# Up-projections of a hybrid attention trunk: split products for fp32, and a plan made from other durations

## The chip, the cores and the metric

The kernel runs on one core of one Trainium2 chip. The metric is the device time of one execution in microseconds (us), as the median of several runs.

## The reference

Two decoder layers work on 256 tokens of width 1024, all in fp32. In each layer the normed input goes through one wide projection (`w_in`), whose parts feed two attentions, NSA (compressed, selected and windowed keys) and MoBA, and two gates. The two attention outputs go through an up-projection each, are gated and summed, and go through `w_out`; a SwiGLU network follows.

```
for l in range(2):
    sh_m, sc_m, g_m, sh_f, sc_f, g_f = split(silu(c) @ w_ada[l] + b_ada[l], 6)
    h = rms_norm(x, norm_mix[l]) * (1.0 + sc_m) + sh_m
    (q_a, ..., q_b, k_b, v_b, g_br) = split(h @ w_in[l], ...)
    y_a = nsa_mixer(...)                       # 256 x 512
    y_b = moba_mixer(q_b, k_b, v_b, ...)       # 256 x 512
    gate_a, gate_b = split(sigmoid(g_br), 2)
    merged = gate_a * (y_a @ w_up_nsa[l]) + gate_b * (y_b @ w_up_moba[l])
    x = x + g_m * (merged @ w_out[l])
    h = rms_norm(x, norm_ffn[l]) * (1.0 + sc_f) + sh_f
    gt, up = split(h @ w_ffn_in[l], 2)
    x = x + g_f * ((silu(gt) * up) @ w_ffn_out[l])
```

## The kernel before, in words

Tokens are handled as two tiles of 128 (`t` = 0, 1), and nearly all time goes into products of a 128x128 piece of activations with a weight tile of 512 columns. Nearly all weights come in units of 128x2048 fp32 values (1 MB) into a tile `raw`. Most products are **split products**: ScalarE makes `hi`, the weights rounded to fp32r, VectorE makes `lo` = `raw` - `hi`, the activations are split alike, and `mm3` issues three fp32r matmuls in place of one fp32 matmul: high by high, high by low, low by high. A unit marked *whole* skips this: `part` multiplies `raw` itself in fp32. Whole are every second block of the lead-in, three units of layer 0, and all up-projections of both layers (`u = load_unit(A[w][l][:, cs_], 4, 512, True)`). The attention output of a token tile, in PSUM tile `y`, is copied to a quarter of the tile `yy` by one `evac` (`whole_piece`), on ScalarE or VectorE.

SBUF holds an arena of 17 tiles of 8 KB per partition. `raw` has the slots 0, 1, 2 (and 11 for some units); `hi` and `lo` have three slots each (and two more for units with `spare`), used by all split weights; `yy` has 11, 12, 13 or 14.

The program first records every operation (`Op`) with a cost in us. `order` then places them on the engines, always the one that can start first, ties by rank. `rounds` repeats this 60 times: each plan is replayed 8 times with random delays of transfers, operations ahead of a wait of TensorE are raised in rank, and the plan with the shortest replay is kept. So the costs written in `_vec`, `act`, `softmax_T` and so on decide the order on each engine, and which of two or three engines takes an operation. Loads go through SyncE's queue in that order; the dot products that make the modulation rows (`aw`, `ada_dot` on VectorE, 80 of them) are loaded and computed far ahead of their use, wherever the plan finds room.

In the last product of the last layer the last output block (token tile 1, columns 512 to 1023) is computed as two halves of 256 columns, so that the first half's residual can be finished while the second half's matmuls run.

Lines of the profile: L662 is a matmul of `term` (all weight products), L648 one of `mm` (attention), L669 a transpose, L583 and L589 VectorE with two tensors (L589 with a scalar too), L601 VectorE with one tensor, L631 ScalarE's `act`, L640 and L641 the two sides of `evac`, L678 a DMA.

Of the kernel before, what the change touches and what calls it, by code (L numbers as in the profile page):

```python
# [17 lines left out]
P = 128  # L18
# [100 lines left out]
class Op:  # L119
    def __init__(self, no, alts, key):  # L120
        self.no, self.alts, self.key = no, alts, key
        self.preds, self.succs, self.acc, self.new = {}, [], [], []
        self.bytes = 0
        self.level = 0.0
        self.stage, self.first, self.boost = None, False, 0.0
        self.func, self.loads, self.parts, self.paced, self.then = None, None, False, False, None
# [5 lines left out]
FIRST = 1000.0  # L132
LAT = {"PE": 0.24, "DVE": 0.09, "ACT": 0.09, "POOL": 0.2, "SP": 0.0, "Q": 0.0}
# [5 lines left out]
class Program:  # L139
# [9 lines left out]
    SWITCH = (0.0, 0.0, 0.1)  # L149
# [116 lines left out]
    def order(self):  # L266
# [24 lines left out]
        parts = False  # L291
# [43 lines left out]
        while left:  # L335
# [6 lines left out]
            for op in ready:  # L342
                if "SP" in op.alts and op.no != loads[0] and (op.paced or self.ops[loads[0]].stage == "lead"):
                    continue
                pl = place(op)
                if pl is None:
                    continue
                for e, (c, _) in op.alts.items():
                    est = max(free[e], pl[0],
                              max((f if q == e else f + LAT[q] for f, q in rt[op.no].values()), default=0.0))  # L350
                    if e == "PE" and op.parts != parts:
                        est = max(est, free[e] + self.SWITCH[0])
                    per.setdefault(e, []).append((est, op, pl[1], c))
# [4 lines left out]
            for e, cs in per.items():  # L358
# [3 lines left out]
                else:  # L362
                    w = eps[e] + (self.SWITCH[1] if e == "PE" else 0.0)
                    pick = max((c for c in cs if c[0] <= t0 + w), key=lambda c: (c[1].rank(e), -c[1].no))
# [38 lines left out]
            if e == "PE":  # L403
                parts = op.parts
# [14 lines left out]
            else:  # L419
                free[e] = t + c  # L420
# [21 lines left out]

    def fill(self, t0, t1):
# [15 lines left out]
        op.stage = "fill"  # L459
# [20 lines left out]
    def replay(self, steps, seed):  # L480
# [4 lines left out]
        dma, table, parts, gaps = 0.0, (), False, []  # L485
        for i, (e, op, c, deps) in enumerate(steps):
# [5 lines left out]
            if e == "PE":  # L492
                if op.stage != "fill" and op.parts != parts:
                    parts = op.parts
                    idle += self.SWITCH[2]
# [13 lines left out]
            free[e] = t + c  # L509
# [49 lines left out]
class Engines:  # L559
# [25 lines left out]
    def stt(self, out, a, s, b, op0, op1, accum=None):  # L585
# [5 lines left out]
                  [a, s, b], [out] + list(kw.values()), extra=0.08 if kw else 0.0)  # L591

    def ttr(self, out, a, b, op0, op1, init, accum):
        self._vec(("DVE",), cols(out), True,
                  lambda v: v.tensor_tensor_reduce(AP(out), AP(a), AP(b), 1.0, init, op0, op1, AP(accum)),  # L595
                  [a, b], [out, accum], extra=0.08)

    def ts(self, out, a, s1, s2, op0, op1=None, engs=("DVE",)):
# [3 lines left out]
                  [a, s1, s2], [out], psum=self._psum(a))  # L602
# [12 lines left out]
    def act(self, out, a, func, scale=None, bias=None, accum=None, late=()):  # L615
# [11 lines left out]
        if accum is not None:  # L627
            kw["accum_out"] = accum
            writes.append(accum)
            c += 0.2  # L630
# [12 lines left out]
    def mm(self, out, lhsT, rhs, start, stop, cost=None):  # L643
# [6 lines left out]
        op.parts = AP(lhsT).shape[0] < P or AP(out).shape[0] < P  # L650

    def term(self, out, lhsT, rhs, first):
# [13 lines left out]
        self.p.op({"PE": (cost, [go])}, [lhsT, rhs], [out], term=s)  # L666

    def tr(self, out, a, ident):
        self.p.op({"PE": (0.109, [lambda: self.nc.tensor.transpose(AP(out), AP(a), AP(ident))])}, [a, ident], [out])  # L669

    def dma(self, out, src, q="SP", least=60000):
# [5 lines left out]
        eng = {"SP": self.nc.sync, "POOL": self.nc.gpsimd}[q]  # L677
        return self.p.op({q: (0.43 if q == "SP" else 0.6, [lambda: eng.dma_start(AP(out), AP(src))])},  # L678
# [7 lines left out]

HALVED = 1
# [15 lines left out]
def trunk_kernel(tc, pools, A):  # L703
# [33 lines left out]
    NB = 17  # L737
# [16 lines left out]
    arena("yy", (11, 12, 13, 14), inturn=True)  # L754
# [373 lines left out]
    def lead_in(bs, h, W):  # L1128
# [16 lines left out]
        dma(vecs, A["vecs"], q="POOL")  # L1145
# [68 lines left out]
    def sublayer_mix(l, h):  # L1214
# [4 lines left out]
        ev, kv_, qv, vv, yv = (R.val(x_) for x_ in ("e", "kk", "qq", "ve", "yy"))  # L1219
# [185 lines left out]
        def softmax_T(s, t, nh, rq_small, cols_, gate):  # L1405
# [21 lines left out]
            alts["ACT"] = (nh * (0.295 + nk / 1200),  # L1427
# [47 lines left out]
        def nsa(t):  # L1475
# [43 lines left out]
            yaT[t] = whole_piece(quarter(yv, t, t), y)  # L1519

        def moba(t):
# [31 lines left out]
            ybT[t] = whole_piece(quarter(yv, 2 + t, 2 + t), y)  # L1553
# [72 lines left out]
        log_soon([yv, *tgv.values()])  # L1626
# [8 lines left out]
    def resid(l, t, c, b, g, e0=0, e1=512):  # L1635
# [3 lines left out]
        with R.ahead():  # L1639
            tt(r, b.of(e0)[:, e0:e1] if e1 - e0 < 512 else b, g[:, cs_], ALU.mult)  # L1640
# [6 lines left out]
    def sublayer_ffn(l, h):  # L1647
# [61 lines left out]
        full = (0, 512)  # L1709
        keys = [(*key, full) for key in keys]  # L1710

        parts = {(t, c): [full] for t in range(NT) for c in range(2)}
        if l == L - 1:
            parts[(NT - 1, 1)] = [(0, 256), (256, 512)]
            keys += [(i, t, k, c, e) for t in range(NT) for c in range(2) for e in parts[(t, c)]
                     for i in range(nu - nl, nu) for k in range(2)]
        else:
            keys += [(i, t, k, c, full) for t in range(NT) for i in range(nu - nl, nu) for k in range(2) for c in range(2)]
        for i, t, k, c, (e0, e1) in keys:
            kk = 2 * i + k  # L1720
            cs_ = slice(c * 512 + e0, c * 512 + e1)
            b = bs[(t, c)]
            if (e0, e1) != full:
                b = b.of(e0)[:, e0:e1]

            R.boost = 20.0 * (4 - 2 * t - c) - e0 / 50 if l == L - 1 and i >= nu - nl else 0.0
            mm3(b, aT[t][kk], us[i].hi[:, k, cs_], us[i].lo[:, k, cs_], kk == 0)
# [73 lines left out]
```

## Time and profile before

| | us |
|---|---|
| runs | 816.85, 816.95, 820.06 |
| median | 816.95 |
| span of the profiled execution | 815.4 |
| around the span (median - span) | 1.55 |
| TensorE busy | 803.8 (99%) |
| VectorE busy | 580.2 (71%) |
| ScalarE busy | 410.3 (50%) |
| DMA moved | 183.82 MB, 225 GB/s |

The span runs from the first to the last event of the program in the profiled execution; the page gives no other time of that execution, so the 1.55 us around it are the difference to the runs. A matmul's duration in a row is longer than its turn on the array, since matmuls overlap; what a kind of matmul costs is read from the distance between starts.

### The profile page before, as it was taken

To read this page: it belongs to the slowest core of one execution; us is meant where nothing else is said; L and a number is where in the kernel's file an instruction comes from. 1 tells how busy PE (TensorE), PEld (TensorE's weight loads), DVE (VectorE), ACT (ScalarE), POOL (GpSimd) and SP (SyncE) were. 2 spreads that over 40 slices of the span, in tenths; PEclk is the share of its full clock that TensorE was granted. 3 is DMA by queue.
4 is the path that set the end of the run, shared out by engine and by line. 5 is a ranking of instruction groups with operands and counts; after the bars stand their busy time and mean duration, and the time that the engine had idled before them with its cause. 6 is when DMAs were issued, how large, how long until landed. Compare 5 with 4: busy or idle time off the path is not lost.

```text
span 815.4 us, 10543 instructions
## 1 busy us (share of the span) xinstructions
PE 803.8 (99%) x3997; PEld 610.0 (75%) x3997; DVE 580.2 (71%) x1025; ACT 410.3 (50%) x654; POOL 79.5 (10%) x75
## 2 busy tenths in 40 slices
PE   8999999999999999999999999999999999999997
PEld 4567656764878888888878887676477888889886
DVE  6889977677986877777788898776377526545454
ACT  5445366662673534433585566587347524433441
POOL 4702620000100000000000442000000000000000
PEclk9999999999999999999999999999999999999999
DMA  9967585538949887977855785540391645555441
GB/s 357 416 230 290 161 295 182 175 130 310 372 152 338 311 305 288 327 293 259 311 174 214 278 289 180 188 151 25 104 344 69 210 153 174 202 192 207 151 158 52
DMA packets 74018, 183.82 MB, mean 225 GB/s; under 512 B 4304, under 2 KB 9696, under 8 KB 73456
## 3 DMA queue, kind: packets, MB, share of 16 engines
q1 hardware_dynamic: 73920, 183.08, 63.0%
q8 instruction: 31, 0.51, 0.2%
q14 instruction: 19, 0.16, 0.1%
q0 software_dynamic: 48, 0.08, 0.0%
HBM read 182.10 MB, written 1.05 MB: 225 GB/s over the span
## 4 chain that ended last, share of the span: by engine, by line
PE 88%; DVE 4%; DMA 2%; ACT 2%; POOL 2%; issue 1%; SPq 0%; DVEq 0%; POOLq 0%
PE bank L662 77%; PE bank L648 6%; PE bank L669 5%; DMA rows<-in_rows 1%; DVE tmp L583 1%; DMA raw<-in_w_out 1%; DVE lo L583 1%; POOL tmp L601 1%; DVE tmp L601 1%; ACT hp L631 1%; ACT hi L631 1%; SPq L678 0%; POOL tmp L583 0%; POOL at L1431 0%; DVE e L583 0%
## 5 line engine op out<-in xcount | busy, mean ns | idle before, releaser
L662 PE MATMUL bank<-hi,hp 128*128 128x512 f32 (+2 forms) x1296 | 359.2, 384 | 2.2 <-DVE hp L583 1.5
L583 DVE TENSOR_TENSOR lo<-raw,hi 128x2048 fp32r<-128x2048 f32 (+2 forms) x107 | 240.4, 2261 | 104.7 <-ACT hi L631 103.8
L631 ACT ACTIVATE hi<-raw 128x2048 fp32r<-128x2048 f32 (+2 forms) x107 | 200.6, 1891 | 223.1 <-PE bank L662 181.9
L662 PEld LDWEIGHTS bank<-hi,hp 128*128 128x128 f32 x1296 | 234.1, 188 | 59.1 <-issue 7.0
L662 PE MATMUL bank<-lo,hp 128*128 128x512 f32 (+2 forms) x648 | 208.2, 383 | 0.3 <-DVE lo L583 0.2
L662 PEld LDWEIGHTS bank<-lo,hp 128*128 128x128 f32 x648 | 119.3, 188 | 24.1 <-issue 2.6
L589 DVE SCALAR_TENSOR_TENSOR aw<-aw,crow 128x1024 f32<-128x1024 f32 x80 | 96.2, 1220 | 7.5 <-DMA aw<-in_w_ada 7.3
L662 PE MATMUL bank<-hi,aT 128*128 128x512 f32 (+1 forms) x364 | 100.7, 387 | 0.0
L662 PEld LDWEIGHTS bank<-hi,aT 128*128 128x128 f32 x364 | 66.6, 188 | 13.5 <-ACT hi L631 1.0
L662 PE MATMUL bank<-raw,yy 128*128 128x512 f32 x128 | 58.7, 596 | 0.7 <-ACT yy L640 0.7
L662 PE MATMUL bank<-lo,aT 128*128 128x512 f32 (+1 forms) x182 | 58.0, 385 | 0.0
L662 PE MATMUL bank<-raw,hd 128*128 128x512 f32 (+1 forms) x112 | 49.6, 568 | 0.9 <-ACT hd L631 0.9
L662 PEld LDWEIGHTS bank<-raw,yy 128*128 128x128 f32 x128 | 23.0, 190 | 23.7 <-issue 21.8
L662 PE MATMUL bank<-hi,mT 128*128 128x512 f32 x128 | 39.9, 403 | 0.1
L662 PEld LDWEIGHTS bank<-lo,aT 128*128 128x128 f32 x182 | 34.1, 188 | 6.1
L669 PE MATMUL bank<-ident,tmp 128*128 128x128 f32 x256 | 37.5, 274 | 1.2 <-DVE tmp L985 0.7
L631 ACT ACTIVATE at<-at,nb,rqa 128x128 f32<-128x128 f32 (+1 forms) x64 | 34.2, 536 | 7.5 <-DVE nb L589 7.5
L669 PEld LDWEIGHTS bank<-ident,tmp 128*128 128x128 f32 x256 | 30.4, 140 | 9.8 <-issue 1.8
L595 DVE CUSTOM_DVE_ANT_0 at<-bank,maskf 128x128 f32<-128x128 f32 (+1 forms) x96 | 29.5, 352 | 11.3 <-PE bank L669 8.9
L662 PEld LDWEIGHTS bank<-raw,hd 128*128 128x128 f32 x112 | 20.6, 189 | 17.2 <-issue 13.4
L583 DVE TENSOR_TENSOR tmp<-tmp,bank 128x512 f32<-128x512 f32 (+1 forms) x24 | 15.1, 639 | 22.0 <-PE bank L662 21.5
L631 ACT ACTIVATE tmp<-bank 128x512 f32<-128x512 f32 (+2 forms) x43 | 20.7, 509 | 16.3 <-PE bank L662 7.0
(185 smaller groups left out, 731.3 us busy)
## 6 DMA issues: line engine op xcount, KB each, us to landing
raw<-in_w_ffn_in SPq DMA_DIRECT2D x44, 1024.0 KB, 6.3
aw<-in_w_ada SPq DMA_DIRECT2D x80, 512.0 KB, 5.7
raw<-in_w_in SPq DMA_DIRECT2D x30, 1024.0 KB, 5.2
raw<-in_w_ffn_out SPq DMA_DIRECT2D x22, 1024.0 KB, 4.9
raw<-in_w_out SPq DMA_DIRECT2D x8, 1024.0 KB, 6.2
raw<-in_w_in SPq DMA_DIRECT2D x8, 908.0 KB, 9.1
sa<-in_w_ada SPq DMA_DIRECT2D x7, 1024.0 KB, 11.9
raw<-in_w_up_nsa SPq DMA_DIRECT2D x4, 1024.0 KB, 6.2
```

Of the source, the lines that this page charges most:

```text
L583: self._vec(engs, cols(out), True, lambda v: v.tensor_tensor(AP(out), AP(a), AP(b), op=op), [a, b], [out])
L589: lambda v: v.scalar_tensor_tensor(AP(out), AP(a), AP(s), AP(b), op0=op0, op1=op1, **{k: AP(x) for k, x in kw.items()}),
L595: lambda v: v.tensor_tensor_reduce(AP(out), AP(a), AP(b), 1.0, init, op0, op1, AP(accum)),
L601: lambda v: v.tensor_scalar(AP(out), AP(a), AP(s1), AP(s2), op0=op0, **kw),
L631: op = self.p.op({"ACT": (c, [lambda: self.nc.scalar.activation(AP(out), AP(a), func, **{k: AP(x) for k, x in kw.items()})])}, reads + lis ...
L648: op = self.p.op({"PE": (cost, [lambda: self.nc.tensor.matmul(AP(out), AP(lhsT), AP(rhs), start=start, stop=stop)])}, [lhsT, rhs], [out])
L662: self.nc.tensor.matmul(AP(out), AP(lhsT), AP(rhs), start=first, stop=v.gone == v.terms)
L669: self.p.op({"PE": (0.109, [lambda: self.nc.tensor.transpose(AP(out), AP(a), AP(ident))])}, [a, ident], [out])
```

## The change

It has five parts. (1) `UPS_WHOLE` is false for both layers, so the eight units of the up-projections are split like the others, and the attention output is split on the way out of PSUM (`y_pieces`): ScalarE writes the high part into `yy`, VectorE the low part into a second `yy` tile (`yl`). (2) The arena gets an 18th tile, first choice for `yy`; the scratch of software DMA is set to 2048 to make room. (3) The matmuls of the last output block run over 512 columns again; only its residual and its store stay in halves. (4) `vecs`, a table of constants of 81.5 KB, is loaded by ScalarE's queue and no longer by GpSimd's. (5) The planner gets other durations: VectorE and ScalarE instructions overlap by `OVER`, an accumulating one costs less, normalising the softmax on ScalarE costs less, VectorE scaling from PSUM by a column costs more, and a change of matmul shape on TensorE costs `TURN`, by row and column class (`forms`).

```diff
+OVER = {"PE": 0.0, "DVE": 0.08, "ACT": 0.1, "POOL": 0.0, "SP": 0.0, "Q": 0.0}
...
-    SWITCH = (0.0, 0.0, 0.1)
+    TURN, SLACK, TALL = 0.15, 0.0, 0.05
+    FLAT, STICK = (P, P), 0.0
...
-            if e == "PE":
-                parts = op.parts
+            if e == "PE" and op.forms:
+                if op.forms[0] != form:
+                    t = max(t, free[e] + self.turn(form, op.forms[0]))
+                form = op.forms[1]
...
-                free[e] = t + c
+                free[e] = t + c - OVER[e]
                 end = t + c
...
-        eng = {"SP": self.nc.sync, "POOL": self.nc.gpsimd}[q]
-        return self.p.op({q: (0.43 if q == "SP" else 0.6, [lambda: eng.dma_start(AP(out), AP(src))])},
+        eng = {"SP": self.nc.sync, "ACT": self.nc.scalar}[q]
+        return self.p.op({q: (0.43 if q == "SP" else 0.15, [lambda: eng.dma_start(AP(out), AP(src))])},
...
+UPS_WHOLE = (False, False)
...
-    NB = 17
+    NB = 18
...
-    arena("yy", (11, 12, 13, 14), inturn=True)
+    arena("yy", (17, 11, 12, 13, 14), inturn=True)
...
-        dma(vecs, A["vecs"], q="POOL")
+        dma(vecs, A["vecs"], q="ACT")
...
-        def whole_piece(d, src):
-            evac(d, src)
-            return [(None, None, d[:, j * P:(j + 1) * P]) for j in range(4)]
+        yl = None if UPS_WHOLE[l] else R.val("yy", dt=F32R)
+
+        def y_pieces(i, src):
+            d = quarter(yv, i, i)
+            if yl is None:
+                evac(d, src)
+                return [(None, None, d[:, j * P:(j + 1) * P]) for j in range(4)]
+            return split_into(d, quarter(yl, i, i), src)
...
-            alts["ACT"] = (nh * (0.295 + nk / 1200),
+            alts["ACT"] = (nh * (0.19 + nk / 1200) + 0.1,
...
-                u = load_unit(A[w][l][:, cs_], 4, 512, True)
+                u = load_unit(A[w][l][:, cs_], 4, 512, UPS_WHOLE[l])
...
-            keys += [(i, t, k, c, e) for t in range(NT) for c in range(2) for e in parts[(t, c)]
-                     for i in range(nu - nl, nu) for k in range(2)]
+            keys += [(i, t, k, c) for t in range(NT) for c in range(2) for i in range(nu - nl, nu) for k in range(2)]
...
-    nc = bacc.Bacc("TRN2", target_bir_lowering=False, num_devices=1)
+    nc = bacc.Bacc("TRN2", target_bir_lowering=False, num_devices=1, dynamic_dma_scratch_size=2048)
```

The order of instructions before and after differs nearly everywhere in its details. Three places matter here. In the names, `hp` is the split normed input, `kk`,`qq` are keys and queries, `pt` softmax weights, `ve` values, `at` softmax rows, `tg` gates, `mT` the gated sum; numbers tell buffers apart. The first place is TensorE in layer 0 at the first up-projections. Before:

```order
L662 MATMUL bank_64<-hi_1047,hp_322 128x512
L662 MATMUL bank_65<-raw_1155,yy_1177 128x512
L662 MATMUL bank_63<-raw_1155,yy_1177 128x512
L669 MATMUL bank_69<-ident_95,at_82 128x128 x4
L648 MATMUL bank_66<-kk_614,qq_682 128x256
...
L648 MATMUL bank_68<-pt_84,ve_772 64x128
L669 MATMUL bank_70<-ident_95,at_81 128x128 x4
L662 MATMUL bank_63<-raw_1155,yy_1177 128x512 x2
L662 MATMUL bank_64<-raw_1211,yy_1177 128x512 x2
L669 MATMUL bank_69<-ident_95,at_83 128x128 x4
```

And after:

```order
L659 MATMUL bank_68<-pt_85,ve_767 64x128
L659 MATMUL bank_68<-pt_84,ve_767 64x128
L678 MATMUL bank_63<-hi_1431,hp_318 128x512
L678 MATMUL bank_64<-hi_1431,hp_321 128x512
...
L678 MATMUL bank_63<-hi_1431,hp_321 128x512
L678 MATMUL bank_65<-hi_1492,yy_1117 128x512
L678 MATMUL bank_65<-lo_1508,yy_1117 128x512
L678 MATMUL bank_64<-hi_1492,yy_1117 128x512
L678 MATMUL bank_64<-lo_1508,yy_1117 128x512
L678 MATMUL bank_64<-hi_1492,yy_1258 128x512
```

Before, fp32 up-projections stand between the attention products of MoBA; after, gate products (`hi_1431`) fill that place, ten of them follow the last attention product, and the split up-projections come behind those, in one block. The second place is VectorE around the same point. Before, from the end of the last softmax:

```order
L613 RECIPROCAL ri_196<-rs_191 128x2
L589 SCALAR_TENSOR_TENSOR aw_74,mod_f_138<-aw_74,crow_101 128x1024
L589 SCALAR_TENSOR_TENSOR aw_72,mod_f_138<-aw_72,crow_101 128x1024
L583 TENSOR_TENSOR gcol_164<-gcol_164,vecs_104 128x8
L589 SCALAR_TENSOR_TENSOR aw_73,mod_f_138<-aw_73,crow_101 128x1024
L589 SCALAR_TENSOR_TENSOR tmp_78<-tg_978,bank_65 128x512
```

And after:

```order
L624 RECIPROCAL ri_196<-rs_191 128x2
L1450 TENSOR_TENSOR at_81<-at_81,ri_196 128x512
L593 TENSOR_TENSOR lo_1508<-raw_1217,hi_1492 128x2048
L652 COPY pt_85<-bank_69 128x512
L652 COPY pt_84<-bank_70 128x512
L593 TENSOR_TENSOR lo_1536<-raw_1260,hi_1516 128x2048
L599 SCALAR_TENSOR_TENSOR aw_72,mod_f_138<-aw_72,crow_101 128x1024
L593 TENSOR_TENSOR yy_1258<-bank_68,yy_1117 128x512
L599 SCALAR_TENSOR_TENSOR aw_73,mod_f_138<-aw_73,crow_101 128x1024
L593 TENSOR_TENSOR lo_1583<-raw_1470,hi_1570 128x2048
```

The low parts of the up-projection weights and of the attention output now stand where modulation dots (`aw`) stood, and fewer dots stand between them. The third place is the end of TensorE's program. Before, after the last transposes of activations:

```order
L669 MATMUL bank_69<-ident_95,tmp_75 128x128 x2
L662 MATMUL bank_66<-lo_5682,aT_5507 128x512
L662 MATMUL bank_66<-hi_5664,aT_5507 128x512 x2
...
L669 MATMUL bank_69<-ident_95,gcol_165 128x128 x4
L662 MATMUL bank_66<-hi_5679,aT_5629 128x256
...
L662 MATMUL bank_68<-hi_5765,aT_5751 128x512 x4
```

And after:

```order
L678 MATMUL bank_65<-lo_5499,hp_4811 128x256
L678 MATMUL bank_64<-lo_5805,aT_5747 128x512
L678 MATMUL bank_64<-hi_5795,aT_5747 128x512 x2
L685 MATMUL bank_69<-ident_95,tmp_76 128x128 x2
L678 MATMUL bank_64<-hi_5795,aT_5747 128x512
L685 MATMUL bank_70<-ident_95,tmp_75 128x128 x2
L678 MATMUL bank_63<-hi_5923,aT_5946 128x512 x2
L678 MATMUL bank_66<-hi_5923,aT_5946 128x512 x2
L678 MATMUL bank_67<-hi_5923,aT_5946 128x512
L678 MATMUL bank_63<-lo_5939,aT_5946 128x512
L685 MATMUL bank_69<-ident_95,gcol_165 128x128 x4
```

Before, matmuls of older activations stand between the last transposes and the first product with their result (`aT_5751`); after, one does, and the SwiGLU's own last matmul (`bank_65`) stands close ahead. After, the four output blocks end one behind another with six or fewer matmuls between the ends.

## Rows read from the trace of the kernel before

**Rows 1.** The page's head, TensorE's busy time with the other engines', and the granted clock of TensorE in 40 slices.

```profile
span 815.4 us, 10543 instructions
PE 803.8 (99%) x3997; PEld 610.0 (75%) x3997; DVE 580.2 (71%) x1025; ACT 410.3 (50%) x654; POOL 79.5 (10%) x75
PEclk9999999999999999999999999999999999999999
```

**Rows 2.** The chain of work that ended last, shares of the span by engine.

```profile
PE 88%; DVE 4%; DMA 2%; ACT 2%; POOL 2%; issue 1%; SPq 0%; DVEq 0%; POOLq 0%
```

**Rows 3.** Busy time of the engines in stretches: the attention of layer 0 up to its `w_out`, its SwiGLU, the same for layer 1, and the end. Columns: stretch and length, then busy us of TensorE, its weight loads, VectorE, ScalarE, GpSimd (with instructions), granted clock, DMA share, GB/s.

```profile
62.00:232.00 170.00, 167.97 (x871) 112.72 (x869) 137.36 (x326) 94.37 (x200) 29.74 (x21) 1.00 0.67 234
232.00:415.00 183.00, 183.00 (x879) 152.37 (x880) 142.45 (x158) 83.95 (x79) 0.00 (x0) 1.00 0.81 291
415.00:627.00 212.00, 210.03 (x1128) 154.99 (x1127) 159.40 (x362) 128.45 (x254) 23.47 (x12) 1.00 0.54 186
```

**Rows 4.** One stretch with VectorE at its fullest, same columns.

```profile
60.00:100.00 40.00, 39.32 (x235) 28.48 (x235) 37.89 (x73) 19.08 (x33) 19.52 (x13) 1.00 0.65 226
```

**Rows 5.** The chain of work in order of time, two long pieces that hold split matmuls alone: start, length in us, what, and how many.

```profile
236.94 72.59 PE bank L662 x319
...
631.94 73.62 PE bank L662 x324
```

**Rows 6.** The fp32 up-projections: the group over the whole span (busy us, mean ns of one | idle before), then two pieces of the timeline (start, length, count). Each fp32 matmul of the program leaves two records.

```profile
L662 PE MATMUL bank<-raw,yy 128*128 128x512 f32 x128 | 58.7, 596 | 0.7 <-ACT yy L640 0.7
```

```profile
172.07 3.60 PE L662 MATMUL bank<-raw,yy 128*128 128x512 f32 x8
...
196.26 6.17 PE L662 MATMUL bank<-raw,yy 128*128 128x512 f32 x14
```

**Rows 7.** Groups of VectorE and ScalarE by shape, with busy us, mean ns of one, and what ended the idle time before them: making `lo`; the low part of an activation from PSUM; softmax normalised; making `hi`; `yy` copied on ScalarE; softmax normalised on ScalarE.

```profile
L583 DVE TENSOR_TENSOR lo<-raw,hi 128x2048 fp32r<-128x2048 f32 x101 | 229.6, 2288 | 101.5 <-ACT hi L631 100.6 <-PE bank L662 0.4
L583 DVE TENSOR_TENSOR aT<-bank,aT 128x512 fp32r<-128x512 f32 x20 | 13.2, 684 | 4.2 <-ACT aT L631 4.2
L1426 DVE TENSOR_TENSOR at<-at,ri 128x512 f32<-128x512 f32 x21 | 14.5, 692 | 0.7
...
L631 ACT ACTIVATE hi<-raw 128x2048 fp32r<-128x2048 f32 x101 | 191.5, 1913 | 219.8 <-PE bank L662 181.9 <-DMA raw<-in_w_out 29.2 <-issue 5.2
L640 ACT ACTIVATE yy<-bank 128x512 f32<-128x512 f32 x6 | 3.6, 597 | 7.1 <-PE bank L648 6.9
L1428 ACT ACTIVATE at<-at,ri 128x256 f32<-128x256 f32 x24 | 10.9, 501 | 3.6 <-DVE nb L589 2.1 <-DVE ri L583 1.2 <-DVE ri L613 0.2
```

**Rows 8.** The modulation dots on VectorE between 145 and 232 us, and `yy` copied by VectorE.

```profile
L589 DVE SCALAR_TENSOR_TENSOR aw<-aw,crow 128x1024 f32<-128x1024 f32 x16 | 19.3, 1218 | 1.2 <-DMA aw<-in_w_ada 1.2
```

```profile
L641 DVE COPY yy<-bank x2: 686/690/693, 134.6 to 163.0; 128x512 f32<-128x512 f32 x2
```

**Rows 9.** Waits of TensorE, longest first: us in total, times, longest.

```profile
PE bank L662 <- DVE hp L583: 1.5, 2, 1.1
PE bank L456 <- DVE zb L808: 1.0, 1, 1.0
PE bank L662 <- ACT hd L631: 0.9, 2, 0.5
PE bank L662 <- ACT yy L640: 0.7, 1, 0.7
```

**Rows 10.** The timeline's end: last transposes, matmuls of 256 columns, VectorE's last residuals.

```profile
799.75 0.60 PE L669 MATMUL bank<-ident,tmp 128*128 128x128 f32 x4
...
803.53 2.77 PE L662 MATMUL bank<-hi,aT 128*128 128x512 f32 x11
...
808.08 0.40 PE L662 MATMUL bank<-hi,aT 128*128 128x256 f32 x2
808.32 0.28 PE L662 MATMUL bank<-lo,aT 128*128 128x256 f32 x1
808.44 0.40 PE L662 MATMUL bank<-hi,aT 128*128 128x256 f32 x2
...
810.60 0.28 PE L662 MATMUL bank<-hi,aT 128*128 128x256 f32 x1
810.92 0.76 DVE L583 TENSOR_TENSOR tmp<-bank,gbc 128x256 f32<-128x256 f32 x2 [0.43 <-PE bank L662]
811.59 0.75 DVE L583 TENSOR_TENSOR x<-x,tmp 128x256 f32<-128x256 f32 x2
```

**Rows 11.** The start: the load of `vecs` on GpSimd, its first and its second use, ScalarE's table load and the instruction behind it; then a piece of the chain.

```profile
0.72 1.28 ACT L631 ACT_TABLE_LOAD   x1 [0.72 <-PEq L1763]
1.43 0.77 POOL L678 DMA_DIRECT2D vecs<-in_vecs  x1
2.57 0.21 ACT L631 ACTIVATE ccol<-ccol 128x8 f32<-128x8 f32 x1 [0.57 <-DMA ccol<-in_c]
7.03 0.29 POOL L605 CAST posf<-vecs 128x3 f32<-128x3 int32 x1
11.46 0.36 DVE L583 TENSOR_TENSOR mod_m<-mod_m,vecs 128x2 f32<-128x2 f32 x2
```

```profile
5.05 11.92 DMA rows<-in_rows
```

More of the change, by code (lines that the diff above doesn't have):

```diff
@@ L125, in __init__ @@
         self.stage, self.first, self.boost = None, False, 0.0
-        self.func, self.loads, self.parts, self.paced, self.then = None, None, False, False, None
+        self.func, self.loads, self.forms, self.paced, self.then = None, None, None, False, None
     def rank(self, e):
@@ L290, in order @@
         table = ()
-        parts = False
+        form = self.FLAT
         parked, aside = {}, set()
@@ L441, in order, with turn @@
         return out
+    def turn(self, a, b):
+        return self.TURN + (self.TALL if b[0] < P <= b[1] else 0.0)
     def fill(self, t0, t1):
@@ L458, in fill @@
             start=True, stop=True)] * n)}, 0.0)
-        op.stage = "fill"
+        op.stage, op.forms = "fill", (self.FLAT, self.FLAT)
         return t0, op
@@ L484, in replay @@
         start, end, by = [], [], []
-        dma, table, parts, gaps = 0.0, (), False, []
+        dma, table, form, gaps = 0.0, (), self.FLAT, []
         for i, (e, op, c, deps) in enumerate(steps):
@@ L492, in replay @@
             if e == "PE":
-                if op.stage != "fill" and op.parts != parts:
-                    parts = op.parts
-                    idle += self.SWITCH[2]
+                if op.forms and op.forms[0] != form:
+                    idle += self.turn(form, op.forms[0])
+                if op.forms:
+                    form = op.forms[1]
                 if idle < self.COLD and op.stage != "fill":
@@ L508, in replay @@
             by.append(who)
-            free[e] = t + c
+            free[e] = t + c - OVER[e]
             if e == "SP":
@@ L601, in ts @@
                   lambda v: v.tensor_scalar(AP(out), AP(a), AP(s1), AP(s2), op0=op0, **kw),
-                  [a, s1, s2], [out], psum=self._psum(a))
+                  [a, s1, s2], [out], psum=self._psum(a),
+                  extra=0.12 if self._psum(a) and isinstance(s1, Ref) else 0.0)
     def copy(self, out, a, engs=("DVE",)):
@@ L649, in mm, with formed @@
                                                                     stop=stop)])}, [lhsT, rhs], [out])
-        op.parts = AP(lhsT).shape[0] < P or AP(out).shape[0] < P
+        self.formed(op, AP(lhsT).shape[0], AP(out).shape[0])
+    @staticmethod
+    def formed(op, k, m):
+        f = tuple(next(w for w in (32, 64, P) if n <= w) for n in (k, m))
+        op.forms = (op.forms[0] if op.forms else f, f)
     def term(self, out, lhsT, rhs, first):
@@ L1552, in moba @@
             R.key = BOOST["moba"][t]
-            ybT[t] = whole_piece(quarter(yv, 2 + t, 2 + t), y)
+            ybT[t] = y_pieces(2 + t, y)
             R.key = 0.0
@@ L1639, in resid @@
         with R.ahead():
[L1640 removed]
+            tt(r, b[:, e0:e1], g[:, cs_], ALU.mult)
             xx = x[t].of(c)
```

45 lines of the change are left out of this document (22 added, 23 removed).

## Prediction, made before the changed kernel ran

> **What bounds the kernel now.** I read the page's head first. TensorE is busy 803.8 of 815.4 us, VectorE 71%, ScalarE 50%, and the granted clock is at its full level in all 40 slices [rows 1], so a saving of TensorE's time need not be paid back through the clock. The chain of work that ended last is 88% TensorE; VectorE, second in it, has 4% [rows 2]. The stretches by stage say where this is strict: in the SwiGLU of layer 0 TensorE is busy 183.00 of 183.00 us, in the attention stages 167.97 of 170 and 210.03 of 212 [rows 3]. The waits confirm it, since the longest group is 1.5 us in two times, and the four longest make 4.1 us together [rows 9]. Whatever leaves TensorE's program therefore shortens the run, as long as what replaces it arrives in time.
>
> A busy share alone could mislead, since matmuls overlap. The two long pieces of the chain decide it: 72.59 us for 319 split matmuls and 73.62 us for 324 are both 0.2275 and 0.2272 us for one [rows 5]. That is one steady turn on the array, without waits. The Trainium skill ("Perfetto Trace Analysis", section "Identifying the Most-Contended Engine") says that matmul busy share is no good measure of TensorE's headroom and that the weight loads' share should be read instead. Here that is 610.0 us, 75% [rows 1], by which a quarter would be free and less matmul work need not shorten the run; the sum by it would be 816.95 us, no change. The constant turn in [rows 5] speaks against it, and it is kept as a rival below.
>
> **The change, part by part.**
>
> *Up-projections split.* They are 64 fp32 matmuls, 128 records [rows 6]. A record's turn comes from the pieces of the timeline: the last of a piece lasts its own 596 ns, so seven turns fill 3.60 - 0.60 us and thirteen fill 6.17 - 0.60, each 0.429 us. One fp32 matmul costs 0.858 us. It becomes three split ones at 0.2275, 0.683 together. The difference is 0.1755, times 64: **-11.2 us**. The Trainium skill ("FP8 and Floating Point Precision", section "TensorE Precision Notes") counts a true fp32 product as four passes, so three in place of four would save a quarter of 64 x 0.858 = 54.9 us, 13.7 us (an estimate), and the sum below would end at 805.5. The rows give a split matmul 0.2275 and a quarter of the fp32 one 0.2145, so I keep 11.2.
>
> *What the split adds on other engines.* Eight more units need `hi`, 8 x 1.913 = 15.3 us of ScalarE, and `lo`, 8 x 2.288 = 18.3 us of VectorE [rows 7]. Eight outputs `y` need a ScalarE and a VectorE pass in place of one: VectorE gets 8 x 0.684 = 5.5 for 2 x 0.690 = 1.4 [rows 7, 8], ScalarE 8 x 0.6 for 6 x 0.597 [rows 7], +1.2. Normalising the softmax moves to ScalarE: VectorE's go from 21 to 17, -2.8, ScalarE's from 28 to 44, at most +8.0 at 501 ns [rows 7]. Net: VectorE +19.6, ScalarE +24.5 at most. This costs nothing if it lies beside TensorE's work. Half of it, 9.8 us, falls in each attention stage. VectorE there goes from 137.36 to 147.2 in a stretch that shrinks to about 164.4 us (90%) in layer 0, and from 159.40 to 169.2 of 206.4 (82%) in layer 1 [rows 3]. The stretch 60 to 100 us shows that TensorE can run 39.32 of 40 us beside a VectorE that is busy 37.89, 95% [rows 4]. There is also room to give: 16 modulation dots, 19.3 us, lie in 145 to 232 us [rows 8], and the SwiGLU behind has 183 - 142.45 = 40.5 us of free VectorE [rows 3]. After, fewer dots stand between the low parts, so the plan does shift them. I take 0; without this cover it is up to 9.8 us a layer. ScalarE mostly waits for TensorE to release buffers, 181.9 of 219.8 us before `hi` [rows 7], so its 24.5 have room.
>
> *Buffers.* The eight units now take turns in the three slots of `hi` and `lo`, with the gates ahead and `w_out` behind them. A unit is ready 1.913 + 2.288 = 4.2 us after it lands at the earliest [rows 7], and 24 split matmuls of a unit last 5.5 us. Three slots cover one unit's preparation; I take 0 here and keep the other end as a rival.
>
> *Waiting for `y`.* Before, TensorE waits 0.7 us for one `yy` [rows 9]. Low parts come a VectorE pass of 0.684 behind the high ones [rows 7]. After the last value product the order puts ten gate matmuls, 10 x 0.2275 = 2.3 us, ahead of the first up-projection in layer 0, and one product by the high part ahead of the first low one. Lower bound 0, upper a `lo` of 2.288 ahead in VectorE's queue and the 0.684 itself for one of the outputs, 3.0. Nearest is the wait that [rows 9] shows, once a layer or a little less: **+1.0**.
>
> *The end, the halves.* 36 matmuls of 256 columns at 0.12 each ([rows 10]: 808.08, 808.32, 808.44) become 18 at 0.2275: 4.3 to 4.1, **-0.2**. But the last block is finished whole. Before, VectorE ends at 812.34, 1.46 us behind the last matmul's end at 810.88 [rows 10]. After, both halves' two steps (0.38 and 0.375 each [rows 10]) follow the last matmul, minus what overlaps, and blocks that end six or fewer matmuls apart (1.4 us) leave steps of 0.69 [rows 7] queued ahead. VectorE then ends some 2.4 us behind TensorE: **+0.9**, bounds 0 and 1.6.
>
> *The end, the last activations.* Before, the transposes of `tmp` start at 799.75 and the product with their result is in the pieces at 803.53 or later [rows 10], with 3.7 us of other matmuls between. After, one matmul stands between the last transposes and that product, which needs a ScalarE copy of the bank, at most 0.6 as `yy`'s [rows 7], and VectorE has a `lo` of 2.288 close by. Bounds 0 and 2.3; I take one ScalarE copy, **+0.6**.
>
> *`vecs` on ScalarE's queue.* GpSimd gives back 0.77 us at 1.43; ScalarE has 0.57 idle ahead of `ccol` at 2.57, which waits for its own transfer [rows 11], so the issue has a hole. What reads `vecs`: GpSimd's `posf` at 7.03 and VectorE's `mod_m` at 11.46 [rows 11]. The rotary path that `posf` feeds waits for `rows`, which lands at 5.05 + 11.92 = 16.97 [rows 11]. 0, bounds -0.4 and +0.4. The price of lateness: VectorE's queue is in order, and `mod_m` stands ahead of the second token tile's norm in the new order, so a `vecs` that lands several us late would hold the norm up.
>
> *Plan and 18th tile.* The costs move nearly every instruction. TensorE's program has no more to win than its idle 815.4 - 803.8 = 11.6 us, of which start and end are part; its four longest wait groups make 4.1 [rows 1, 9]. On the other side a reshuffled order can lose as much. I take 0, bounds -4 and +4. The 18th tile holds the low half of `yy` and sets no other work free; 0.
>
> **Sum.** 815.4 - 11.2 - 0.2 + 0.9 + 0.6 + 1.0 = 806.5 us of span. The median of the runs lies 816.95 - 815.4 = 1.55 above the profiled span, so 806.5 + 1.55 = **808.0 us**.
>
> **The rivals.** For this kernel 0.5%, about 4.1 us, is what a measurement can tell from no change: faster means below 812.9, slower above 821.0.
>
> *The plan wins too.* It removes most of the 4.1 us of waits of [rows 9] and the additions of 2.5 us above don't appear: 802 to 805.5. For it: the 60 rounds keep the shortest replay, now with durations nearer to [rows 7]. Against: little is left to win.
>
> *VectorE becomes the bound in an attention stage.* At 90% of layer 0's stage [rows 3], with softmax chains in it that can't be shifted, 4 to 10 us come back: 812 to 818. For it: 37.89 of 40 in 60 to 100 [rows 4]. Against: TensorE lost only 0.68 us there, and 19.3 us of dots can go [rows 8].
>
> *Slower: the units' buffers.* Each up-projection unit waits for a slot of `lo` that the unit ahead frees only when its matmuls end, so its 2.288 us on VectorE lies open: 8 x 2.288 = 18.3, 808.0 + 18.3 = 826 us. It decides from a wait of (821.0 - 808.0)/8 = 1.6 us a unit; from 1.1 the gain is gone. For it: ScalarE's `hi` wait 181.9 us for TensorE [rows 7], so slots are short already. Against: split units run 72.59 us at the steady turn with the same slots [rows 5].
>
> *TensorE is not the bound*, so taking its time away does nothing: 816.9, as the weight loads' share would have it; [rows 3, 5] speak against it.
>
> **How the numbers follow.** Forecast 0.62 (805.5 to 811, as the additions reach their lower or upper bounds in part); the plan wins too 0.15; VectorE the bound 0.15; buffers 0.05; TensorE not the bound 0.03. Faster takes the first two and the lower third of the VectorE case, 0.05: 0.82. Same takes 0.09 of that case and 0.03: 0.12. Slower is the buffers' 0.05 and 0.01 of VectorE in both layers: 0.06. The range 802.5 to 814 leaves out some 0.03 below, and above it 0.08 of the VectorE case, the buffers and the unbound TensorE.
>
> **What would show it.** TensorE's groups: `raw` by `yy` gone, 192 split ones with `yy`, and TensorE's busy time about 11 us lower, with split pieces of the chain still at 0.2275 a matmul. The stretch up to layer 0's `w_out` some 5.6 us shorter, and layer 1's too; the SwiGLU stretches unchanged. `lo` at 109 instead of 101. Waits of TensorE for `lo` or `yy` of a few tenths, none repeated eight times. At the end VectorE some 2.4 us behind the last matmul, and a wait for `aT` or `lo` under 1 us. The forecast is wrong if TensorE waits for `lo` once a unit, if VectorE's softmax steps end TensorE's idle time in 60 to 232 us, if the start is late for `vecs`, or if a split matmul with `yy` takes more than 0.2275 us a turn.

## The result, and the profile after

The changed kernel takes 812.72 us (median of 8 runs, 811.34 to 813.78), beside 817.99 us for the kernel before in the same series. The ratio is 0.993 with a 95% interval of 0.991 to 0.995: faster by 5.3 us, where 8.95 were forecast. The forecast was 808.0 us, so 4.7 us are missing. In the profiled executions the span fell from 815.4 to 809.6 us, by 5.8, where the sum made it 806.5; the profiled execution after took 811.34 us, 1.4 less than the median, so 3.1 of the missing 4.7 us can be looked for in it.

The page's head after ([rows 1] before):

```profile
span 809.6 us, 10657 instructions
PE 793.1 (98%) x4040; PEld 619.6 (77%) x4040; DVE 594.6 (73%) x1027; ACT 431.5 (53%) x685; POOL 74.3 (9%) x73
```

TensorE is busy 10.7 us less, close to the 11.4 of the forecast (11.2 + 0.2). But it stands idle 809.6 - 793.1 = 16.5 us, for 11.6 before: 4.9 more. Less work and more idle time make the 5.8. To see where the idle time lies, both spans are cut alike. Columns as in [rows 3]; length less TensorE's busy time is idle time. Before:

```profile
0.00:40.00 40.00, 36.99 (x135) 21.46 (x136) 29.44 (x64) 18.89 (x31) 24.29 (x40) 1.00 0.96 386
40.00:100.00 60.00, 59.32 (x313) 41.55 (x312) 53.84 (x110) 29.71 (x56) 21.56 (x15) 1.00 0.65 226
100.00:232.00 132.00, 130.54 (x648) 85.33 (x646) 101.42 (x259) 76.22 (x170) 10.21 (x8) 1.00 0.68 239
440.00:630.00 190.00, 188.43 (x1015) 137.74 (x1014) 140.54 (x326) 111.82 (x221) 22.83 (x12) 1.00 0.51 177
```

After:

```profile
0.00:40.00 40.00, 37.45 (x136) 21.80 (x137) 30.37 (x63) 20.04 (x34) 23.23 (x39) 1.00 0.97 390
40.00:100.00 60.00, 54.40 (x295) 38.08 (x295) 53.25 (x107) 28.95 (x55) 24.43 (x17) 1.00 0.71 240
100.00:232.00 132.00, 129.94 (x695) 94.08 (x694) 114.22 (x274) 88.51 (x186) 5.18 (x5) 1.00 0.73 256
440.00:630.00 190.00, 189.49 (x1073) 147.86 (x1073) 151.54 (x331) 125.85 (x240) 20.38 (x11) 1.00 0.55 188
```

From 40 to 100 us the idle time goes from 0.68 to 5.60 us, +4.9, as much as in the whole span. The small changes elsewhere (-0.5 at the start, +0.6 in 100 to 232, -1.1 in 440 to 630, +0.3 and +0.5 in the two stretches that are left out) cancel. VectorE's busy time in 40 to 100 us is no longer than before (53.25 for 53.84), and no up-projection stands there. So it is not the added low parts that hold TensorE up. The chain shows the same from the other side. Its first piece of split matmuls in layer 0's SwiGLU starts at 231.90 us before and 231.49 after, so layer 0 kept 0.4 of its 5.6 us; all the rest of the gain comes behind it. Before:

```profile
231.90 3.93 PE bank L662 x16
```

After:

```profile
231.49 4.83 PE bank L678 x20
...
625.44 73.95 PE bank L678 x325
```

The second piece, 73.95 us for 325, is 0.2275 us for a split matmul, as before [rows 5]. TensorE's waits, longest first ([rows 9] before; us in total, times, longest):

```profile
PE bank L685 <- DVE kbd_tok L611: 1.7, 1, 1.7
PE bank L678 <- DVE hp L593: 1.7, 3, 0.8
PE bank L659 <- DVE e L593: 1.5, 1, 1.5
PE bank L685 <- DVE tmp L593: 1.1, 3, 0.5
PE bank L678 <- ACT hd L642: 1.1, 2, 0.7
...
PE bank L685 <- ACT e L651: 0.9, 2, 0.7
PE bank L659 <- ACT ve L642: 0.6, 1, 0.6
```

`kbd_tok` (the compressed keys of NSA), `e` (the input of its small network), `ve` (values) and two of the three waits for `tmp` (queries and keys after their rotation) belong to the preparation of layer 0's attention, between 57 and 97 us. These seven waits are the whole 5.6 us; 4.1 us of them are for VectorE, 1.5 for ScalarE.

The groups that carry the terms, after ([rows 6, 7] before): the up-projections, `lo`, the low half of the attention output.

```profile
L678 PE MATMUL bank<-hi,yy 128*128 128x512 f32 x128 | 40.1, 396 | 0.0
L678 PE MATMUL bank<-lo,yy 128*128 128x512 f32 x64 | 23.8, 390 | 0.0
L593 DVE TENSOR_TENSOR lo<-raw,hi 128x2048 fp32r<-128x2048 f32 x109 | 250.6, 2316 | 111.7 <-ACT hi L642 111.2
L593 DVE TENSOR_TENSOR yy<-bank,yy 128x512 fp32r<-128x512 f32 x8 | 5.5, 687 | 1.6 <-ACT yy L642 1.1 <-PE bank L678 0.5
```

The up-projections are 192 matmuls with no idle time ahead of them, so none of them waits for `yy`. The end, after ([rows 10] before):

```profile
798.10 1.43 PE L678 MATMUL bank<-hi,aT 128*128 128x512 f32 x5 [0.25 <-ACT aT L642]
...
804.35 0.39 PE L678 MATMUL bank<-hi,aT 128*128 128x512 f32 x1
805.22 0.75 DVE L593 TENSOR_TENSOR tmp<-bank,gbc 128x256 f32<-128x256 f32 x2
805.89 0.75 DVE L593 TENSOR_TENSOR x<-x,tmp 128x256 f32<-128x256 f32 x2
```

VectorE ends at 806.64, 1.90 us behind the last matmul's end at 804.74; before it was 1.46.

### The profile page after: what moved, and what is told of

Read it like the earlier page. It is cut to its first block, busy times and chain, and to the rows that moved or that the text cites. A ratio compares the mean times of both kernels' runs of the same rounds, so it can differ in the third digit from the quotient of the medians.

```text
span 809.6 us, 10657 instructions
## 1 busy us (share of the span) xinstructions
PE 793.1 (98%) x4040; PEld 619.6 (77%) x4040; DVE 594.6 (73%) x1027; ACT 431.5 (53%) x685; POOL 74.3 (9%) x73
## 4 chain that ended last, share of the span: by engine, by line
PE 68%; DVE 4%; ACT 1%; issue 1%; DVEq 0%; ACTq 0%
PE bank L678 62%; PE bank L685 4%; PE bank L659 2%; DVE lo L593 1%; DVE tmp L593 1%; ACT at L642 1%; ACT hp L642 0%; DVE tmp L611 0%; DVE aw L599 0%; DVE at L605 0%; DVE ss L620 0%; DVE x L593 0%; DVE mT L599 0%; ACT pt L651 0%; ACT at L1452 0%
## 5 line engine op out<-in xcount | busy, mean ns | idle before, releaser
L678 PE MATMUL bank<-hi,hp 128*128 128x512 f32 (+2 forms) x1296 | 364.6, 384 | 2.0 <-DVE hp L593 1.7
L593 DVE TENSOR_TENSOR lo<-raw,hi 128x2048 fp32r<-128x2048 f32 (+2 forms) x115 | 261.4, 2289 | 115.0 <-ACT hi L642 114.5
L642 ACT ACTIVATE hi<-raw 128x2048 fp32r<-128x2048 f32 (+2 forms) x115 | 215.4, 1892 | 216.0 <-PE bank L678 194.4
L678 PE MATMUL bank<-lo,hp 128*128 128x512 f32 (+2 forms) x648 | 215.2, 384 | 0.0
L678 PE MATMUL bank<-hi,aT 128*128 128x512 f32 x352 | 101.2, 395 | 0.3 <-ACT aT L642 0.3
L678 PE MATMUL bank<-lo,aT 128*128 128x512 f32 x176 | 57.1, 392 | 0.0
L678 PE MATMUL bank<-hi,yy 128*128 128x512 f32 x128 | 40.1, 396 | 0.0
L593 POOL TENSOR_TENSOR tmp<-tmp,tmp 128x512 f32<-128x512 f32 (+2 forms) x12 | 14.0, 1167 | 195.2 <-DVE tmp L599 174.8
```

The source lines that it names most:

```text
L593: self._vec(engs, cols(out), True, lambda v: v.tensor_tensor(AP(out), AP(a), AP(b), op=op), [a, b], [out])
L642: op = self.p.op({"ACT": (c, [lambda: self.nc.scalar.activation(AP(out), AP(a), func, **{k: AP(x) for k, x in kw.items()})])}, reads + lis ...
L678: self.nc.tensor.matmul(AP(out), AP(lhsT), AP(rhs), start=first, stop=v.gone == v.terms)
```

## The experiments

All were planned anew, so each has an order of its own, and the idle times of each are those of one profiled execution. The kernel before took 817.5 to 817.9 us beside them. The question is the 4.9 us in 40 to 100 us: knock-on of the split, effect of the planner's new durations, or an accident of one plan.

**Up-projections whole again.**

```diff
-UPS_WHOLE = (False, False)
+UPS_WHOLE = (True, True)
```

> The changed kernel with all up-projections whole (fp32) again, the other four parts kept, planned anew. In the changed kernel's profile TensorE stands idle 5.6 us between 40 and 100 us (0.7 before), which is about what the forecast lacks. Theory V (knock-on of the split: its low parts fill VectorE later, so modulation dots are pulled into 40 to 100 us, where VectorE is full): without the split that idle time falls under 1.5 us, and undoing the split costs only 11.0 - 4.5 = 6.5 us, about 819 us. Theory D (the new durations make the planner order VectorE too tightly there) and theory S (an accident of one plan): the idle time does not depend on the split; by D it stays near 5 us and the time is 812.7 + 11 = 824 us.

820.81 us, ratio 1.0044 (1.0027 to 1.0060). The idle time stays:

```profile
40.00:100.00 60.00, 53.70 (x293) 37.77 (x292) 53.37 (x105) 29.68 (x56) 26.36 (x20) 1.00 0.69 238
```

That is 6.3 us without any split up-projection, where the knock-on theory wanted less than 1.5, so it falls. (The profiled execution took 825.27 us, 4.5 above the median; how much of that lies in this stretch is not shown, but 1.8 us would be left in any case.) The rest of the change without the split is slower than the kernel before, by 3 us; with the new durations the split is worth 820.8 - 812.7 = 8.1 us.

**Old durations, all else kept.**

```diff
-OVER = {"PE": 0.0, "DVE": 0.08, "ACT": 0.1, "POOL": 0.0, "SP": 0.0, "Q": 0.0}
+OVER = {"PE": 0.0, "DVE": 0.0, "ACT": 0.0, "POOL": 0.0, "SP": 0.0, "Q": 0.0}
...
-                  [a, s, b], [out] + list(kw.values()))
+                  [a, s, b], [out] + list(kw.values()), extra=0.08 if kw else 0.0)
...
-            c += 0.1
+            c += 0.2
...
-            alts["ACT"] = (nh * (0.19 + nk / 1200) + 0.1,
+            alts["ACT"] = (nh * (0.295 + nk / 1200),
...
-                    idle += self.turn(form, op.forms[0])
+                    idle += 0.1
```

(and, in the order itself, no price for a turn; the replay's 0.1 us still goes by the new classes of shapes, so the durations are not quite those of the kernel before)

> The changed kernel planned with the durations of the kernel before (no overlap on VectorE and ScalarE, the old costs of accumulating instructions and of the softmax on ScalarE, 0.1 us for a turn in the replay alone). Theory V: no change, 811.5 to 814 us, idle TensorE between 40 and 100 us still 4 to 6 us. Theory D: the idle time falls under 1.5 us and the time to about 808 us. Theory S: anything within 4 us of 812.7, with the idle time at other places.

821.22 us, ratio 1.0039 (1.0027 to 1.0051): slower than the kernel before, with the split in it. The idle time in 40 to 100 us is gone:

```profile
40.00:100.00 60.00, 59.32 (x310) 40.91 (x308) 53.24 (x110) 29.58 (x57) 21.55 (x15) 1.00 0.65 224
```

So the new durations do cause that idle time, as theory D has it; but its time was wrong by 13 us, since something larger shows up late in both attentions. The planner fills foreseen gaps of TensorE with matmuls of zeros (`zb`), which count as busy. Two groups, 160 to 232 us and 560 to 630 us (busy, mean ns | idle before):

```profile
L465 PE MATMUL bank<-zb 128*128 128x512 bf16 x16 | 3.9, 379 | 0.0
...
L465 PE MATMUL bank<-zb 128*128 128x512 bf16 x8 | 2.2, 382 | 0.0
```

The timeline of TensorE at the end of layer 0's MoBA, this kernel:

```profile
182.53 1.09 PE L659 MATMUL bank<-pt,ve 128*64 128x128 f32 x14 [0.33 <-ACT pt L651]
183.55 0.66 PE L685 MATMUL bank<-ident,at 128*128 128x128 f32 x4
184.04 1.67 PE L465 MATMUL bank<-zb 128*128 128x512 bf16 x7
185.56 0.65 PE L685 MATMUL bank<-ident,at 128*128 128x128 f32 x4
186.14 0.43 PE L659 MATMUL bank<-pt,ve 128*64 128x128 f32 x2
186.90 1.09 PE L659 MATMUL bank<-pt,ve 128*64 128x128 f32 x14 [0.32 <-ACT pt L651]
187.91 0.66 PE L685 MATMUL bank<-ident,tmp 128*128 128x128 f32 x4
188.41 1.46 PE L465 MATMUL bank<-zb 128*128 128x512 bf16 x6
190.47 0.50 PE L678 MATMUL bank<-hi,yy 128*128 128x512 f32 x1 [0.60 <-ACT yy L642]
```

Transposes of the last softmax rows, value products and zeros alternate; no useful matmul stands between them: the gate products are used up, and the next up-projections wait for `yy`, which comes out of these value products. In the kernel before, the slow fp32 up-projections stand at that place (the first place shown of the order). After, the gate products do, the last value product starts at 175.35 us, 11 us sooner than here, and the changed kernel has no zeros behind 100 us:

```profile
175.35 1.09 PE L659 MATMUL bank<-pt,ve 128*64 128x128 f32 x16
176.37 0.73 PE L678 MATMUL bank<-hi,hp 128*128 128x512 f32 x2
```

**Other random numbers in the planner's replays, twice.**

```diff
-            runs = [self.replay(steps, seed) for seed in range(self.RUNS)]
+            runs = [self.replay(steps, seed) for seed in range(100, 100 + self.RUNS)]
```

(200 in place of 100 the second time)

> The changed kernel with the planner's replays drawn from other random numbers, nothing else. Theories V and D: 811.5 to 814 us, TensorE idle 4 to 6 us between 40 and 100 us, since the cause lies in the work or in the durations. Theory S: the time moves by 1.5 us or more, and the idle time of that stretch by 2 us or more.

> As the run before, with a third set of random numbers. V and D: 811.5 to 814 us and 4 to 6 us idle in 40 to 100 us. S: the three plans spread over 3 us or more, and the idle time stands at other places.

813.35 us (0.9946, 0.9934 to 0.9958) and 810.98 us (0.9918, 0.9905 to 0.9931). Plans of one kernel spread over 2.4 us, but all three have 5.6 us of idle time in 40 to 100 us, and none has late zeros. That idle time is no accident; differences of 2 us between two plans prove nothing.

**The fourth corner: whole up-projections and old durations** (both edits above).

> The changed kernel with whole up-projections and with the old durations: only the 18th tile, the load of vecs on ScalarE's queue and the last block in one piece are left of the change. With the old durations the split kernel took 821.2 us and its plan holds 28 filler matmuls of zeros late in both attentions, where the kernel before has none. Theory C (cover: the long fp32 up-projections were what TensorE did while the last softmax chains ran, and the split takes that work away): this one has no such fillers and takes 817 to 819 us, so the split alone, under the old durations, costs some 3 us. Rival (the 3.4 us come from the load of vecs or from the end): 820 to 822 us here too.

819.75 us, ratio 1.0024 (1.0015 to 1.0033), no late zeros, 0.66 us idle in 40 to 100 us. The expectation was 817 to 819; its 28 fillers of the split kernel count four that lie before 100 us, 24 are late. Only the up-projections differ from the second experiment, and at the place of its zeros they stand in fp32:

```profile
179.99 0.60 PE L685 MATMUL bank<-ident,at 128*128 128x128 f32 x4
180.43 1.02 PE L678 MATMUL bank<-raw,yy 128*128 128x512 f32 x2
181.38 1.09 PE L659 MATMUL bank<-pt,ve 128*64 128x128 f32 x16
```

So it is the split that takes the cover away. What is left of the change (end, `vecs`, 18th tile, the classes of shapes) gains nothing; the 1.9 us by which it is slower may be no more than a new draw of the plan, and which part costs them was not tried.

**Old durations with the split, second draw.**

> The split kernel with the old durations and other random numbers in the planner's replays. Theory C: again over 818 us, with 4 us or more of fillers and waits in the last parts of the two attentions. Rival (the first was one bad plan): 811 to 816 us.

824.26 us, ratio 1.0084 (1.0069 to 1.0099), again with zeros late in both attentions (3 and 14), and with 5.8 us of idle time in 100 to 232 us. The four corners, then:

| | old durations | new durations |
|---|---|---|
| whole up-projections | 817.9 (before), 819.75 | 820.8 |
| split up-projections | 821.2, 824.3 | 812.7, 813.35, 810.98 |

Only both together make the kernel faster. The split alone makes it slower, but its two draws differ by 3.1 us, so its price is known no better than as 1 to 5 us over 819.75. The new durations alone gain nothing; the 1.1 us over 819.75 is less than draws of one kernel differ by.

**Which duration.** Four kernels take up the lines of the second experiment in part. First, the overlap alone is old:

```diff
-OVER = {"PE": 0.0, "DVE": 0.08, "ACT": 0.1, "POOL": 0.0, "SP": 0.0, "Q": 0.0}
+OVER = {"PE": 0.0, "DVE": 0.0, "ACT": 0.0, "POOL": 0.0, "SP": 0.0, "Q": 0.0}
```

> The changed kernel with only the overlap of VectorE's and ScalarE's instructions (0.08 and 0.1 us) set back to nothing in the planner; the other new durations stay. Theory D in its narrow form (the overlap makes the planner think VectorE free between 40 and 100 us, so dots and transposes stand too early there): TensorE's idle time in that stretch falls from 5.6 to under 1.5 us, the late stretches stay as in the changed kernel, 808 us. Rival (the overlap is also what moves the softmax ahead and saves the late stretches): idle time or fillers of 4 us or more come back behind 160 us, 812 to 821 us.

811.72 us (0.9926, 0.9912 to 0.9940). The idle time in 40 to 100 us falls to 2.3, but in layer 1 it goes from 0.5 to 3.6 us:

```profile
40.00:100.00 60.00, 57.74 (x305) 39.75 (x304) 53.27 (x101) 29.17 (x54) 21.48 (x15) 1.00 0.60 217
...
440.00:630.00 190.00, 186.38 (x1056) 145.19 (x1055) 156.97 (x335) 122.70 (x230) 27.39 (x13) 1.00 0.53 181
```

The early idle time had a real price: without it the last matmul of layer 0's `w_out` starts at 222.78 us, 3.9 us sooner than in the changed kernel (226.71) and 4.7 sooner than before (227.49). In this kernel, in the changed one, and before:

```profile
222.78 0.40 PE L678 MATMUL bank<-hi,mT 128*128 128x512 f32 x1
```

```profile
226.71 0.49 PE L678 MATMUL bank<-hi,mT 128*128 128x512 f32 x1
```

```profile
227.49 0.39 PE L662 MATMUL bank<-hi,mT 128*128 128x512 f32 x1
```

From there to the end of the span it takes 586.2 us, the changed kernel 582.8, the kernel before 587.9. So this plan has most of layer 0's gain and little of what follows; the changed kernel has the reverse. What it loses in layer 1 is another wait: GpSimd normalises softmax rows there, and TensorE waits for them.

```profile
PE bank L685 <- POOL at L1455: 2.0, 2, 1.5
```

Whether that belongs to the missing overlap or to this one plan is not shown.

Second, the softmax price alone is old:

```diff
-            alts["ACT"] = (nh * (0.19 + nk / 1200) + 0.1,
+            alts["ACT"] = (nh * (0.295 + nk / 1200),
```

> The changed kernel with only the old price of normalising the softmax on ScalarE. If this price is what keeps the late stretches free (the softmax goes to ScalarE, 17 passes on VectorE instead of 25), 3 us or more of idle time come back behind 140 us: 815 to 819 us, and the 40 to 100 us stretch stays at 5 to 6 us idle. Rival (the overlap does it): 811 to 814 us.

812.16 us (0.9933, 0.9920 to 0.9945): no change, no zeros behind 100 us, 4.6 us idle in 40 to 100 us. The softmax price is not what keeps the late stretches free.

Third, all durations old, but the turn is new. Against the kernel of the second experiment this is

```diff
-                    idle += 0.1
+                    idle += self.turn(form, op.forms[0])
```

and the same price in the order.

> The split kernel with all durations old but the price of a change of matmul shape on TensorE (0.15 or 0.2 us, also while the order is made), which stays new. With all durations old the split took 821.2 and 824.3 us, with 24 filler matmuls late in the attentions; this plan has 8. Theory C by steps (each new duration moves the softmax chains ahead of the gate products a little, none is needed alone): between the two, 815 to 819 us. Rival (the turn does it all): 811 to 814 us. Rival (the turn does nothing): 820 us or more.

816.71 us (0.9987, 0.9977 to 0.9997); 8 zeros late, 0.67 us idle in 40 to 100 us.

Fourth, all old, but the overlap is new. Against the kernel of the second experiment:

```diff
-OVER = {"PE": 0.0, "DVE": 0.0, "ACT": 0.0, "POOL": 0.0, "SP": 0.0, "Q": 0.0}
+OVER = {"PE": 0.0, "DVE": 0.08, "ACT": 0.1, "POOL": 0.0, "SP": 0.0, "Q": 0.0}
```

> The split kernel with all durations old but the overlap of VectorE's and ScalarE's instructions, which stays new. 15 late fillers in the plan, all in layer 1, where up-projections stand between the value products as in the kernel before. Theory C by steps: 815 to 819 us, layer 0's late stretch free, layer 1's not. Rival (the overlap does it all): 811 to 814 us; it also should bring the idle 5 us of 40 to 100 us if that comes from the overlap, and under 2.5 us if it does not.

817.00 us (0.9992, 0.9983 to 1.0001); 15 zeros, all in layer 1, and the early idle time is here:

```profile
40.00:100.00 60.00, 54.56 (x294) 37.72 (x293) 51.70 (x97) 28.28 (x56) 25.05 (x18) 1.00 0.66 234
```

Each of the two alone, in one plan each, brings some 4 to 8 us of what the old durations lose, neither all of it; and neither the overlap nor the softmax price is missed where it alone is taken away. The turn alone was not taken away. Over all kernels the early idle time goes with the overlap: 3.9 to 6.3 us in the eight that plan with it, 0.7 to 2.3 us in the six that don't (the kernel before among these).

**Through which instruction?** Two tries. The power on GpSimd that scales the compressed keys:

```diff
-            E_.raw("POOL", 1.2, lambda: nc.gpsimd.tensor_tensor(AP(r)[:64], ...
+            E_.raw("POOL", 2.4, lambda: nc.gpsimd.tensor_tensor(AP(r)[:64], ...
```

> The changed kernel with one planner price more set to what the trace shows: the power on GpSimd that makes the compressed keys' scale (rc, planned at 1.2 us, 1.9 us in the profile before and 2.9 after) at 2.4 us. Theory G (TensorE's wait of 1.7 us for kbd_tok comes from this price): that wait falls under 0.5 us, and the time by 1 to 2 us, to 811 us. Rival (VectorE's queue is late there in any case): the wait goes to the next instruction, 812 to 814 us, and idle TensorE in 40 to 100 us stays at 5 us or more.

814.39 us (0.9965, 0.9952 to 0.9978), 1.7 us over the changed kernel, less than its draws differ by. TensorE's wait for `kbd_tok` falls from 1.7 to 0.9 us, not under 0.5, and its idle time in 40 to 100 us to 3.9. But 4.3 us of idle time appear in layer 1, in 440 to 500 us, where it waits for another scale (in the profiled execution, which took 816.54 us, 2.2 above the median):

```profile
PE bank L685 <- DVE rkb L611: 2.1, 1, 2.1
...
PE bank L685 <- DVE kbd_tok L611: 0.9, 1, 0.9
```

The dots are asked for more slowly:

```diff
-ADA_PACE = [(1.5, 1.5, 1.0), (0.7, 0.7, 0.3)]
+ADA_PACE = [(1.2, 1.2, 1.2), (0.7, 0.7, 0.3)]
```

> The changed kernel with layer 0's modulation dots asked for more slowly (1.2 a unit for 1.5). The order has no dot ahead of kbd_tok instead of one, and fewer before the first softmax. Theory of the dots (those that the plan pulls into 40 to 100 us, 5.35 us of VectorE for 1.23 before, are what keeps VectorE late): VectorE's dots there fall by 2 us or more and TensorE's idle time from 5.6 to under 4 us, 810 to 811.5 us. Rival (the dots are only fill, and the late chain is GpSimd's and ScalarE's): idle time stays at 5 us or more, 812 to 814 us.

812.38 us (0.9939, 0.9927 to 0.9952). The dots in 40 to 100 us fall from 5.35 to 3.50 us of VectorE, and TensorE's idle time there stays at 5.7 us:

```profile
40.00:100.00 60.00, 54.26 (x295) 37.44 (x295) 54.42 (x120) 29.73 (x57) 27.14 (x17) 1.00 0.67 234
```

The dots are not the cause, and the price of the power is at most a part of it. That planning with the overlap brings the early idle time is shown; by which instruction it comes stays open. No kernel of these beats the changed one by more than its plans spread.

## Why the prediction was right, and where it was not

The time lies in the range and on the forecast side, above the likeliest case (805.5 to 811).

- **Up-projections, -11.2.** Right: 192 split matmuls, the turn unchanged at 0.2275 us, TensorE's busy time down 10.7.
- **Added work of VectorE and ScalarE, 0.** Right: 109 `lo` in place of 101, `yy` at 687 ns, and no matmul with them waits. Between 100 and 232 us VectorE rose by 12.8 us while TensorE's idle time rose by 0.6.
- **Buffers, 0.** Right: no wait for a unit's `lo`; the slower rival did not come.
- **Waiting for `y`, +1.0.** Too much: no up-projection waits. In layer 0 gate products stand between the last value product and the first up-projection.
- **The end.** Too much: VectorE ends 1.90 us behind TensorE, not 2.4 (+0.44 for +0.9), and the wait for the last activations is 0.25 us, not 0.6.
- **`vecs`, 0.** Right: ScalarE issues it at 0.71 us, VectorE's first use at 5.91 us has no wait ahead of it, and the first 40 us lose 0.5 us of idle time.
- **Plan, 0 with bounds of -4 and +4.** The step that failed: +4.9 us of idle time in 40 to 100 us, beyond the bound, most of it in the stretch that [rows 4] shows. The prediction took TensorE's 39.32 of 40 us there as proof that a full VectorE is harmless. It was harmless in that order only: after, VectorE is no busier there (53.25 of 60 us for 53.84), and TensorE waits all the same, four times for a result of VectorE and three times for one of ScalarE. This term alone is larger than the 3.1 us of span that are missing; the smaller additions made up for the rest.
- **VectorE the bound, 812 to 818.** The time and the place are this rival's, its mechanism is not: the idle time is there without the split, and with VectorE no busier than before.
- **What no step had.** The sum took away the fp32 matmuls as work and not as cover. They were what TensorE did while the last softmax chains ran; with the old durations the split kernel pays for that with 6.1 us of late zeros and with waits, and gains nothing of the 11 us. In the plans made with all the new durations the last chains end sooner and gate products stand at that place; there the gain comes through. The prediction saw those gate products in the order and used them for the wait for `y` alone.

## What to carry to other kernels

A slow instruction on the bounding engine may be the cover of another engine's chain: before its saving is booked, name what will stand in its place while that chain runs. Where a planner sets the order, parts of a change don't add; two parts done singly and together (four kernels) tell more than any part undone. And plans of the same kernel drawn anew give the spread, here 2.4 us between three draws of one and 3.1 us between two of another; a smaller difference between two plans can't be told from a new draw.

## What was not expected of the hardware

A small VectorE instruction can last several times its usual time while GpSimd works. In the changed kernel `kbd_tok` (32x64, usually 0.24 us) lasts 1.38 us. VectorE:

```profile
90.17 1.38 DVE L611 TENSOR_SCALAR kbd_tok<-tmp,rc 32x64 f32<-32x64 f32 x1 [0.44 <-POOL rc L1412]
...
92.63 0.24 DVE L611 TENSOR_SCALAR kbd_tok<-tmp,rc 32x64 f32<-32x64 f32 x1
```

GpSimd at that time:

```profile
90.10 0.72 POOL L593 TENSOR_TENSOR st<-rows,nsin 128x256 f32<-128x256 f32 x1
90.79 0.71 POOL L593 TENSOR_TENSOR ct<-rows,sincos 128x256 f32<-128x256 f32 x1
```

The long one ends at 91.55, just behind the end of GpSimd's two passes at 91.50; the short one runs beside a power on GpSimd alone. The like stands in six more profiles of the experiments: all eight of these instructions that last over 1.1 us, and one of 0.60, end 0.05 us behind the end of a GpSimd pass that is no power. It isn't the whole rule: four of 0.61 to 0.62 us, one of them in the kernel before, end 0.15 to 0.16 us behind the start of such a pass, with the pass still running. That the one waits for the other is read from the times, and wasn't tried by itself. Nor is it what holds TensorE up in 40 to 100 us: in the kernel with slower dots all four last 0.25 us or less, and TensorE is idle there for 5.7 us.
